# Second attention's and retention's queries and keys: from turned projections to projections by tokens, turned through HBM

## The chip, the cores and the metric

One NeuronCore of a Trainium2 chip runs the whole program. The metric is device microseconds from the start of the program to its end, the median of three runs. Nothing is shared with other cores; HBM is read and written by this core's 16 DMA engines alone.

## The reference

Two layers (D = 1024, 256 tokens, float32), each a mixer and an MLP. The mixer projects the normalised input once into thirteen pieces and feeds three branches:

```python
p = rms_norm(x, g) @ w_in
cq, ckv, k_rope, mq, mk, mv, rq, rk, rv, rg, g_mla, g_moba, g_ret = split(p)
o_mla  = mla_branch(cq, ckv, k_rope, ...)             # first attention, 8 heads
o_moba = moba_branch(mq, mk, mv, cos, sin)            # second attention, 8 heads of 64, partial rotary
o_ret  = retention_branch(rq, rk, rv, rg, ..., cos, sin)   # retention, 4 heads of 64, full rotary
x = x + (sigmoid(g_mla) * (o_mla @ w_a) + sigmoid(g_moba) * (o_moba @ w_b) + sigmoid(g_ret) * (o_ret @ w_c)) @ w_out
x = x + squared_relu(rms_norm(x, g2) @ w_up) @ w_down
```

The change concerns `mq`, `mk` (256 tokens x 512 columns each) and the pair `rq, rk` (together 512 columns): how they are projected, scaled by each token's 1/rms, brought into a layout with the head dimension on the partitions (what the scores need), and rotated (`x1*cos - x2*sin`, `x1*sin + x2*cos`: each element needs its partner from the other half of the rotary dimension).

## The kernel before, in words

**Arithmetic.** Every fp32 product is three TensorE passes: both operands are split into a high part (fp32r) and a low rest, and hi x hi, lo x hi and hi x lo are added in one PSUM bank. Weights arrive by SP's DMA queue as 512 KB tiles `raw` (L218), ScalarE makes the high part `whi` (L284), VectorE the rest `wlo` (L286). There are 7 `raw` tiles and 6 each of `whi` and `wlo`, filled in the order of `weight_plan`.

**Two ways to project.** *By tokens* (`project`, matmuls at L305 to L307, weights moving): 128 activations' columns are loaded into the array, 512 weight columns stream past; for 256 tokens, 512 columns and 8 slices of D that is 2 x 8 x 3 = 48 matmuls of 512 columns, into two `acc` banks. *Turned* (`project_turned`, weights loaded, L504 to L526): for each of 4 blocks of 128 columns, 8 matmuls at L520 stream the high and low parts of 256 tokens side by side (512 columns), and 8 at L522 the high part against `wlo` (256 columns). Both ways stream the same 24,576 columns. In layer 0 `mq` shares the start-up loop over the 8 slices of D with the first attention's columns (`start`; L897 and L899 are its turned matmuls, L905 to L908 the other branch's).

**What a turned projection needs after.** Each block is joined from the two halves of its bank: ScalarE copies one (`second`, L502), VectorE adds (`qkraw`, L502). Tokens are on the free axis, so 1/rms is needed as a row: `stats_row` turns it with TensorE (L456, two transposes a layer) and copies it (`rrow`, L445), and `tables` multiplies it into the rotary tables (`tab`, L533). Rotary partners lie 32 partitions away; `swapped` (L544) copies them with four DMAs of 64 KB within SBUF per pair of blocks. GpSimd rotates the second attention's (`rope_turned`, L556 and L559), VectorE retention's (L1123, L1124).

**The order of the work.** Units of the program (`prog`) stand in a list, extra steps are hung on units with `at(slot(unit, n), ...)`, and a scheduler with its own timeline gives every engine one fixed order; `behind`, `issue_after` and `keep_in_program_order` pin single instructions. An engine executes its order strictly, and so does SP, which issues nearly all DMAs: an issue that waits holds back every later one. The mixer's units run: `start` or `b0`/`mq`, `mk`, then `mv` with the first attention's up-projections between (`qrope`, `qnope`, `kvup`), the gates `gmla`, `gmoba`, then `rqk`, `rv`, `rg`, `gret`, the branch projections, `w_out`. The softmax work of both attentions (L604 to L627, probabilities turned through HBM by L659 and L667) is spread over VectorE and ScalarE under the gates and retention's projections. The first attention's queries `Q` (L1033, L1034) wait for a rotary part `qr` (L1012) and its partner copies `qkoth<-qr` (L544 too); its scores are L1057. Retention's scores are L591 into `ps_r`, read by L1139 into `retA`, used by `ret_values` (L1147 to L1149, `por`).

**Turning through HBM** exists already for the MLP: VectorE transposes 32 x 32 blocks (L335, `hblocks`), one 512 KB DMA writes them to a scratch tensor in HBM (`bounce`, L349), four DMAs of 128 KB read them back turned (`hturned`, L355).

Of the kernel before, what the change touches and what calls it, by code (L numbers as in the profile page):

```python
# [14 lines left out]
P = 128  # L15
# [57 lines left out]
def weight_plan():  # L73
# [7 lines left out]
    def turned(key, cols):  # L81
        for n in range(4):
            block((*key, n), "w_in", KD, cols[P * n : P * n + P], KD)

# [3 lines left out]
    for l in range(L):  # L88
        if l == 0:

            for i in range(2):
                plan.append(((l, "mq", i), "w_in", (0, 1), C_MQ[256 * i : 256 * i + 256]))
            plan.append(((l, "b0", 0), "w_in", (0, 1), C_MLA))
            for k in range(1, KD):
                plan.append(((l, "b0mq", k), "w_in", (k, 1), [*C_MLA, *C_MQ]))
        else:
            block((l, "b0"), "w_in", KD, C_MLA, 2)
            turned((l, "mq"), C_MQ)
        turned((l, "mk"), C_MK)
# [15 lines left out]
        turned((l, "rqk"), C_RQK)  # L115
# [41 lines left out]
def trunk(ctx: ExitStack, tc: tile.TileContext, gx, wts, consts, gfin, gn, xtok, out):  # L157
# [113 lines left out]
    def fetch(key):  # L271
# [10 lines left out]
        parts = (slice(0, 416), slice(416, sz)) if key[1] == "b0mq" else (slice(0, sz),)  # L282
# [82 lines left out]
    class Normed:  # L365
# [87 lines left out]

    def along_free(r, pb):
        for t in range(NT):
            nc.tensor.transpose(pb[:, S + P * t : S + P * t + P], r[:, t : t + 1].to_broadcast([P, P]), ident)  # L456
        return pb[:, S : 2 * S]
# [29 lines left out]
    def project_t(l, key, n, xn, o):  # L487

        wh, wl = load_w(l, key, n, 0)
        for k in range(KD):  # L490
            xh, xl = xn.k(k)
            three(o, wh[:, k, :], wl[:, k, :], xh, xl, k == 0, k == KD - 1)

    def joins(done):

        pair = []

        def join(n, acc):
            if n % 2 == 0:
                pair.append(w2k("qkraw"))  # L500
            second = sb.tile([P, S], F32, name="second", tag="relu", bufs=3)
            both = nc.scalar.copy(second, acc[:, S : 2 * S]), nc.vector.tensor_add(  # L502
                halves(pair[-1])[:, n % 2, :], acc[:, 0:S], second
            )  # L504
            if n % 2:
                done(n // 2, pair[-1])
            return both

        return join

    def project_turned(l, key, xn, done):


        join = joins(done)

        def unit(n):
            wh, wl = load_w(l, key, n, 0)
            acc = acc_tile()
            for k in range(KD):
                nc.tensor.matmul(acc, wh[:, k, :], xn.both(k), start=k == 0, stop=False)  # L520
            for k in range(KD):
                nc.tensor.matmul(acc[:, 0:S], wl[:, k, :], xn.k(k)[0], start=False, stop=k == KD - 1)  # L522
            joined = join(n, acc)
            if key == "rqk" and n:
                behind[l, *(("rv", 3), ("rg", 0), ("rope",))[n - 1]] = joined

        for n in range(4):
            prog.append(((key, n), lambda n=n: unit(n)))

    def tables(xn, tab, engine):  # L530

        o = sb.tile([P, 2 * S], F32, name="tab", bufs=1)
        mul = engine.tensor_mul(halves(o), halves(tab), xn.row[:, None, :].to_broadcast([P, 2, S]))  # L533
        if engine is nc.vector:
            tc.keep_in_program_order(mul)
        return o
# [11 lines left out]

    def rope_turned(raw, tab, engine, late=False):

        other = swapped(raw, late)
        o = sb.tile([P, 2 * S], F32, name="qkT", bufs=4)
        cos, sin = (tab[:, S * i : S * i + S][:, None, :].to_broadcast([P, 2, S]) for i in range(2))
        jobs = [(engine, halves(o), halves(raw), cos), (nc.gpsimd, halves(other), halves(other), sin)]
        for on, *operands in jobs[::-1] if late else jobs:
            mul = on.tensor_mul(*operands)  # L556
        if late:
            tc.keep_in_program_order(mul)
        engine.tensor_add(o, o, other)  # L559
        return halves(o)  # L560
# [216 lines left out]
    begin((0, "mq", 0), "w2k", W2K, nc.scalar)  # L777
    begin((0, "mq", 1), "w2k", W2K)
# [17 lines left out]
    begin((0, "mk", 0, 0))  # L796
# [28 lines left out]
    def layer(l, xn, before):  # L825
# [52 lines left out]
        def start(k, mq):  # L878

            if k == 0:  # L880
                b0.extend(misc_tile("b0") for _ in range(NT))
                mq.extend(acc_tile() for _ in range(4))
            before(k)
            ah, al = xn.k(k)
            if k == 0:
                ws = [load_w(l, "mq", i) for i in range(2)]
                wq = [[w[:, 0, P * i : P * i + P] for w in two] for two in ws for i in range(2)]
                wb = [w[:, 0, :] for w in load_w(l, "b0", 0)]
            else:
                w = load_w(l, "b0mq", k)  # L890
                wq = [[part[:, 0, 416 + P * n : 416 + P * n + P] for part in w] for n in range(4)]
                wb = [part[:, 0, 0:416] for part in w]

            def turned_part(part, ns):
                for n in ns:
                    if part == 0:
                        nc.tensor.matmul(mq[n], wq[n][0], xn.both(k), start=k == 0, stop=False)  # L897
                    else:
                        nc.tensor.matmul(mq[n][:, 0:S], wq[n][1], ah, start=False, stop=k == KD - 1)  # L899
# [10 lines left out]
            if k < KD - 1:  # L910

                for part in range(2):
                    for job in (turned_part, b0_part) if k == 0 else (b0_part, turned_part):
                        job(part, range(4)) if job is turned_part else job(part)
            else:

                join = joins(moba_pair("mq"))
                for part in range(2):
                    turned_part(part, [0])
                for part in range(2):  # L920
                    b0_part(part)
                for n in range(1, 4):
                    for part in range(2):
                        turned_part(part, [n])

                have(1)
                for n in range(4):
                    behind[l, "mk", 1, 0] = behind[l, "mk", 2, 0] = join(n, mq[n])
# [3 lines left out]
        def moba_pair(key):  # L932
            def done(i, raw):
                mqkv[key, i] = raw

            return done

        def moba_tables():
            mqkv["tab"] = tables(xn, TAB, nc.vector)

        def moba_rope(key, i):
            qkT[key][i] = rope_turned(mqkv[key, i], mqkv["tab"], nc.gpsimd, l == 0)

        if l:
            project_turned(l, "mq", xn, moba_pair("mq"))
# [5 lines left out]
            at(slot("mq", 2), xn.stats_row)  # L951
        else:
# [7 lines left out]
            at(slot("start", KD - 1), xn.stats_row)  # L960
        project_turned(l, "mk", xn, moba_pair("mk"))
# [81 lines left out]
        at(slot("mk", 1) if l else slot("gmla0", 1), moba_tables)  # L1043
# [703 lines left out]
```

## Time and profile before

| | us |
|---|---|
| median of 3 runs (lowest, highest) | 803.86 (803.32, 804.36) |
| span of the profiled execution | 801.8 |
| TensorE busy | 795.0 (99% of the span) |
| VectorE busy | 672.4 (84%) |
| ScalarE busy | 489.7 (61%) |
| GpSimd busy | 72.4 (9%) |

The profiler's span covers the instructions; a timed run of this kernel lasts 2.1 us longer by the median (803.86 less 801.8). The granted TensorE clock reads 9 (90% or more) in all 40 slices of the span. Busy TensorE time is that of overlapping matmuls: the distance of one start to the next (227 ns in a run of 512-column matmuls) is what a matmul costs, not its mean duration of 390 ns.

### The profile page before, as it was taken

The page shows a single profiled execution, that of the slowest core. Times are in us where ns is not written, and L with a number is a line of the kernel's source. Part 1 is how long each engine was busy: PE and PEld are TensorE (multiplying, and loading weights), DVE is VectorE, ACT ScalarE, POOL GpSimd, SP SyncE. Part 2 cuts the span into 40 slices and gives each one's busy share as a digit, 9 for nine tenths or more (in the row PEclk, how much of TensorE's full clock was granted, in tenths as well). Part 3 has the DMA queues.
Part 4 walks back from the last instruction along what each step waited for, and adds up shares of the span by engine and source line. Part 5 has one row for each costly group of instructions (what it writes and reads, how often), then busy time and mean ns, then how long its engine had stood idle before and what let it go on. Part 6 is the DMA issues. An engine that isn't in the chain of part 4 may idle for free.

```text
span 801.8 us, 11409 instructions
## 1 busy us (share of the span) xinstructions
PE 795.0 (99%) x3915; PEld 665.1 (83%) x3915; DVE 672.4 (84%) x1128; ACT 489.7 (61%) x758; POOL 72.4 (9%) x61
## 2 busy tenths in 40 slices
PE   9999999999999999999999999999999999999997
PEld 7888887888888888888898888888888888888885
DVE  6859998978888888887798987888698878899785
ACT  7786664653557666666486756655545666667562
POOL 0200810000030000000024330000000300000000
PEclk9999999999999999999999999999999999999999
DMA  9975788975677776787747689687665678788751
GB/s 337 344 238 193 233 270 295 269 264 171 218 232 236 270 214 251 256 271 225 252 149 240 184 231 328 226 261 241 218 221 190 193 259 280 228 284 324 260 174 54
DMA packets 68411, 192.12 MB, mean 240 GB/s; under 512 B 8320, under 2 KB 24832, under 8 KB 68352
## 3 DMA queue, kind: packets, MB, share of 16 engines
q1 hardware_dynamic: 67776, 190.52, 72.5%
q10 hardware_dynamic: 576, 0.87, 0.3%
q8 instruction: 31, 0.51, 0.3%
q14 instruction: 28, 0.23, 0.1%
HBM read 168.81 MB, written 18.87 MB: 234 GB/s over the span
## 4 chain that ended last, share of the span: by engine, by line
PE 98%; ACT 1%; DVE 1%; issue 0%; DVEq 0%
PE acc L305 17%; PE acc L307 17%; PE acc L306 17%; PE pup L306 8%; PE pup L305 8%; PE pup L307 8%; PE acc L1304 6%; PE acc L520 4%; PE acc L522 2%; PE ps_s L1057 1%; PE acc L897 1%; PE po L685 1%; PE ps_s L591 1%; PE warm L805 0%; PE acc L899 0%; PE po L687 0%
## 5 line engine op out<-in xcount | busy, mean ns | idle before, releaser
L284 ACT ACTIVATE whi<-raw 128x1024 fp32r<-128x1024 f32 (+3 forms) x263 | 265.0, 1020 | 165.8 <-PE acc L307 89.9
L286 DVE TENSOR_TENSOR wlo<-raw,whi 128x1024 fp32r<-128x1024 f32 (+3 forms) x263 | 315.9, 1218 | 55.1 <-ACT whi L284 54.1
L305 PE MATMUL acc<-whi,xs 128*128 128x512 f32 (+1 forms) x304 | 119.4, 394 | 0.2 <-DVE qkraw L502 0.2
L306 PE MATMUL acc<-wlo,xs 128*128 128x512 f32 (+1 forms) x304 | 117.8, 388 | 0.0
L307 PE MATMUL acc<-whi,xs 128*128 128x512 f32 (+1 forms) x304 | 117.6, 388 | 0.0
L306 PE MATMUL pup<-wlo,xs 128*128 128x512 f32 x256 | 99.8, 390 | 0.0
L307 PE MATMUL pup<-whi,xs 128*128 128x512 f32 x256 | 99.6, 389 | 0.0
L305 PE MATMUL pup<-whi,xs 128*128 128x512 f32 x256 | 99.4, 389 | 0.0
L307 PE MATMUL acc<-whi,sq 128*128 128x512 f32 x184 | 71.8, 390 | 0.0
L305 PE MATMUL acc<-whi,sq 128*128 128x512 f32 x184 | 71.8, 390 | 0.0
L306 PE MATMUL acc<-wlo,sq 128*128 128x512 f32 x184 | 71.6, 389 | 0.0
L305 PEld LDWEIGHTS acc<-whi,xs 128*128 128x128 f32 x304 | 57.0, 188 | 13.0 <-issue 0.8
L307 PEld LDWEIGHTS acc<-whi,xs 128*128 128x128 f32 x304 | 57.1, 188 | 11.3
L306 PEld LDWEIGHTS acc<-wlo,xs 128*128 128x128 f32 x304 | 57.1, 188 | 10.8
L307 PEld LDWEIGHTS pup<-whi,xs 128*128 128x128 f32 x256 | 48.0, 188 | 9.9
L306 PEld LDWEIGHTS pup<-wlo,xs 128*128 128x128 f32 x256 | 48.1, 188 | 9.8
L305 PEld LDWEIGHTS pup<-whi,xs 128*128 128x128 f32 x256 | 47.9, 188 | 9.9
L613 ACT ACTIVATE prob<-prob,smx 128x128 f32<-128x128 f32 x64 | 28.3, 444 | 30.3 <-DVE smx L610 30.3
L396 POOL TENSOR_TENSOR sqsum<-sqsum,xsq 128x256 f32<-128x256 f32 x16 | 18.2, 1139 | 310.7 <-DVE sqsum L394 298.7
L307 PEld LDWEIGHTS acc<-whi,sq 128*128 128x128 f32 x184 | 34.5, 188 | 7.7 <-DVE sq L326 0.6
L520 PE MATMUL acc<-xs,whi 128*128 128x512 f32 x160 | 40.6, 393 | 0.0
L306 PEld LDWEIGHTS acc<-wlo,sq 128*128 128x128 f32 x184 | 34.5, 188 | 7.2
(277 smaller groups left out, 1383.0 us busy)
## 6 DMA issues: line engine op xcount, KB each, us to landing
raw<-wts SPq DMA_DIRECT2D x264, 512.0 KB, 5.2
bounce<-hblocks SPq DMA_DIRECT2D x16, 512.0 KB, 3.8
hturned<-bounce SPq DMA_DIRECT2D x64, 128.0 KB, 3.1
pbounce<-blocks SPq DMA_DIRECT2D x8, 768.0 KB, 5.9
probT<-pbounce SPq DMA_DIRECT2D x32, 192.0 KB, 5.6
qkoth<-qkraw SPq DMA_DIRECT2D x48, 64.0 KB, 4.7
raw<-wts SPq DMA_DIRECT2D x5, 464.0 KB, 6.0
raw<-wts SPq DMA_DIRECT2D x4, 416.0 KB, 4.8
```

The lines of the kernel that those rows point to most:

```text
L284: fetched.append(nc.scalar.activation(hi[:, cs], raw[:, cs], AF.Copy))
L286: nc.vector.tensor_sub(lo[:, cs], raw[:, cs], hi[:, cs].bitcast(F32))
L305: nc.tensor.matmul(o, ah, bh, start=start, stop=False, **more)
L306: nc.tensor.matmul(o, ah, bl, start=False, stop=False, **more)
L307: nc.tensor.matmul(o, al, bh, start=False, stop=stop, **more)
L396: (nc.gpsimd if n < self.on_pool else nc.vector).tensor_add(self.sum, self.sum, sq)
L520: nc.tensor.matmul(acc, wh[:, k, :], xn.both(k), start=k == 0, stop=False)
L522: nc.tensor.matmul(acc[:, 0:S], wl[:, k, :], xn.k(k)[0], start=False, stop=k == KD - 1)
L591: mm = nc.tensor.matmul(bank[:, o], a[rows, sa], b[rows, sb_], start=True, stop=True)
L613: nc.scalar.activation(p[:, a:b], p[:, a:b], AF.Exp, bias=m[:, 2 + i : 3 + i], scale=d**-0.5, accum_out=m[:, 4 + i : 5 + i])
L685: nc.tensor.matmul(dst, vh, pT[h + j][0], start=True, stop=False)
L1304: nc.tensor.matmul(o, a, b, start=half == 0 and i == 0, stop=4 * half + n == KD and i == len(jobs) - 1)
```

## The change

The six turned projections (`mq`, `mk`, `rqk` in both layers) become projections by tokens. Their weights are now blocked like the others (two slices of D by 512 columns). ScalarE copies the two finished banks out with the token's 1/rms as the scale (`rows`, L881 and L1053 of the new file), VectorE transposes 32 x 32 blocks (L331), one DMA writes 512 KB to HBM (L478), and eight of 128 KB read it back (L483): four give the turned matrix (`raw`), four the same with neighbouring groups of 32 exchanged (`oth`, the rotary partners). `stats_row`, `tables`, `joins` and the SBUF partner copies of these three go; the partner copies of the first attention's `qr` stay. The rotation is done on the re-read matrices with unscaled tables. Of the pins by `behind` around `mk`, `rv`, `rg` and the rotations, most go.

```diff
-        turned((l, "mk"), C_MK)
+        block((l, "mk"), "w_in", KD, C_MK, 2)
...
-        turned((l, "rqk"), C_RQK)
+        block((l, "rqk"), "w_in", KD, C_RQK, 2)
...
-        def stats_row(self):
-
-            pb = along_free(self.r, self.ps)
-            self.row = sb.tile([P, S], F32, name="rrow", bufs=1)
-            nc.scalar.activation(self.row, pb, AF.Copy)
...
-            for k in range(KD):
-                nc.tensor.matmul(acc, wh[:, k, :], xn.both(k), start=k == 0, stop=False)
-            for k in range(KD):
-                nc.tensor.matmul(acc[:, 0:S], wl[:, k, :], xn.k(k)[0], start=False, stop=k == KD - 1)
-            joined = join(n, acc)
...
+    def exchanged(rows, name, tags):
+
+        blocks = blocks_tile(name)
+        for t in range(NT):
+            turn_row(blocks, t, rows[t])
+        bounce = dr.tile([P, 4 * S], F32, name="bounce", bufs=2)
+        nc.sync.dma_start(bounce, blocks)
+        both = [wp.tile([P, 4 * S], F32, name=name + part, tag=tag, bufs=1) for part, tag in zip(("raw", "oth"), tags)]
+        for flip, dst in enumerate(both):
+            for b in range(4):
+                src = bounce.rearrange("(a p) (b r) -> b p a r", a=4, b=4)[b ^ flip]
+                nc.sync.dma_start(dst[32 * b : 32 * b + 32, :].rearrange("p (a r) -> p a r", a=4), src)
+        return both
...
+            def mq_part(part):
+                for a in (ah, al) if part == 0 else (ah,):
+                    for t in range(NT):
+                        first, stop = k == 0 and part == 0 and a is ah, k == KD - 1 and part == 1
+                        nc.tensor.matmul(mq[t], a[:, P * t : P * t + P], wq[part], start=first, stop=stop)
...
+        def exchange(key, accs):
+
+            rows = [w2k("rows") for _ in range(NT)]
+            for t in range(NT):
+                nc.scalar.activation(rows[t], accs[t], AF.Copy, scale=xn.col[t])
+            mqkv[key] = exchanged(rows, key, ("tsums", "thi") if key == "mk" else ("tlo", "exch"))
...
-            project_turned(l, "mq", xn, moba_pair("mq"))
+            project(l, "mq", xn, 512, lambda accs: exchange("mq", accs))
...
-        project_turned(l, "mk", xn, moba_pair("mk"))
+        project(l, "mk", xn, 512, lambda accs: exchange("mk", accs))
...
-                at(slot("mk", 1 + 2 * i), lambda i=i: moba_rope("mq", i))
+                at(slot("mv", 2 * i), lambda i=i: moba_rope("mq", i))
...
-        project_turned(l, "rqk", xn, ret_pair)
-        at(slot("rqk", 1), ret_tables)
+        project(l, "rqk", xn, 512, ret_exchange)
```

Counted over the program, TensorE loses 192 turned matmuls of 512 columns (160 at L520, 32 at L897), 192 of 256 (160 at L522, 32 at L899) and 4 transposes, and gains 288 of 512. VectorE loses 24 additions and 4 table products and gains 12 block transposes; ScalarE loses 24 copies of 128 x 256 and 2 of a row and gains 12 of 128 x 512. SP loses 48 copies of 64 KB and gains 6 writes of 512 KB and 48 reads of 128 KB. GpSimd has as many rotations as before.

The scheduler moves other work with it. SP's queue in layer 1, from the last weights of the keys to the first softmax's turning, before (`qkoth<-qr` are the partners of the first attention's queries, `qkoth<-qkraw` those of the second's):

```order
L544 DMA qkoth<-qkraw 32x512 x4
L218 DMA raw<-wts 128x1024 x2
L544 DMA qkoth<-qkraw 32x512 x4
L218 DMA raw<-wts 128x1024 x2
L544 DMA qkoth<-qr 32x512 x4
L218 DMA raw<-wts 128x1024 x6
```

and with the change:

```order
L478 DMA bounce<-mqblocks 128x1024
L483 DMA mqraw<-bounce 32x4x256 x4
L483 DMA mqoth<-bounce 32x4x256 x4
L213 DMA raw<-wts 128x1024 x4
L478 DMA bounce<-mkblocks 128x1024
L213 DMA raw<-wts 128x1024
L483 DMA mkraw<-bounce 32x4x256 x4
L483 DMA mkoth<-bounce 32x4x256 x4
L509 DMA qkoth<-qr 32x512 x4
L213 DMA raw<-wts 128x1024 x9
```

The partners of the first attention's queries now stand behind the write of the second attention's keys and all eight reads of it. On VectorE in layer 0, where retention's queries and keys come out, before (`prob`, `smx`, `blocks` are the softmax, `omlal` the first attention's output):

```order
L502 TENSOR_TENSOR qkraw<-acc,second 128x256
L627 STREAM_TRANSPOSE blocks<-prob 128x3x4x32 x2
L1123 TENSOR_TENSOR qkoth<-qkoth,tab 128x512
L1123 TENSOR_TENSOR qkT<-qkraw,tab 128x512
L1124 TENSOR_TENSOR qkT<-qkT,qkoth 128x512
L286 TENSOR_TENSOR wlo<-raw,whi 128x1024 x2
L326 TENSOR_TENSOR omlal<-po,omlah 128x512 x2
```

and with the change, first where the blocks are transposed, then, behind four scores' softmax, where the rotation stands:

```order
L282 TENSOR_TENSOR wlo<-raw,whi 128x1024 x6
L331 STREAM_TRANSPOSE rqkblocks<-rows 128x4x4x32 x2
L579 STREAM_TRANSPOSE blocks<-prob 128x3x4x32 x2
L322 TENSOR_TENSOR omlal<-po,omlah 128x512 x2
...
L499 TENSOR_TENSOR qkT<-rqkraw,dec 128x512 x2
L574 TENSOR_SCALAR prob<-prob,smx 128x128
L574 TENSOR_SCALAR prob<-prob,smx 128x256
L568 RECIPROCAL smx<-smx 128x2
L499 TENSOR_TENSOR rqkoth<-rqkoth,dec 128x4x4x32
```

The rotation moved from ahead of that softmax's scores into the middle of its normalisation; retention's scores on TensorE moved with it, from the middle of `rg` to the first matmul behind `rg`.

## Rows read from the trace of the kernel before

**Rows 1.** The page: busy time by engine, and the chain by engine.

```profile
PE 795.0 (99%) x3915; PEld 665.1 (83%) x3915; DVE 672.4 (84%) x1128; ACT 489.7 (61%) x758; POOL 72.4 (9%) x61
...
PE 98%; ACT 1%; DVE 1%; issue 0%; DVEq 0%
```

**Rows 2.** The chain of waits, 24 to 52 us: start, length, what.

```profile
25.52 1.85 PE acc L520 x8
27.37 0.95 PE acc L522 x8
...
44.88 0.66 PE pct L975 x6
```

**Rows 3.** Two stretches of TensorE: length, busy time (records), clock, DMA share, GB/s.

```profile
25.52:36.69 11.17, 11.17 (x65) 1.00 0.89 293
36.69:44.88 8.19, 8.19 (x38) 1.00 1.00 388
```

**Rows 4.** TensorE's timeline from 115 to 119 us, then the chain there.

```profile
117.55 0.50 PE L305 MATMUL acc<-whi,xs 128*128 128x512 f32 x1 [0.24 <-DVE qkraw L502]
...
117.16 0.35 DVE qkraw L502
```

**Rows 5.** The joins of the turned blocks (tile second): ns min/median/max, first and last start.

```profile
L502 ACT COPY second<-acc x24: 351/372/396, 23.2 to 514.3; 128x256 f32<-128x256 f32 x24
L502 DVE TENSOR_TENSOR qkraw<-acc,second x24: 409/418/425, 23.6 to 515.5; 128x256 f32<-128x256 f32 x24
```

**Rows 6.** ScalarE copying a 512-column bank; VectorE's block transposes; their write's landing.

```profile
L1108 ACT ACTIVATE rv<-acc,ms x4: 668/670/673, 139.5 to 531.8; 128x512 f32<-128x512 f32 x4
...
L335 DVE STREAM_TRANSPOSE hblocks<-relu x32: 666/704/714, 243.8 to 771.4; 128x512 f32<-128x512 f32 x32
...
DMA to landing us min/median/max: 2.6/3.8/5.0
```

**Rows 7.** SP's waits (total, times, longest); its issues of turned reads and their landing.

```profile
SPq L355 <- DMA bounce<-hblocks: 50.9, 16, 4.6
...
L355 SPq DMA_DIRECT2D hturned<-bounce x64: 318/423/1785, 248.9 to 776.1; - x64
...
DMA to landing us min/median/max: 2.5/3.1/4.6
```

**Rows 8.** VectorE's timeline, 38 to 46 us: the first attention's latent, layer 0.

```profile
39.59 1.24 DVE L864 TENSOR_SCALAR c<-c,ssc,ms 128x256 f32<-128x256 f32 x4
```

**Rows 9.** The first attention's rotary queries (tile qr): ns min/median/max, landing.

```profile
L544 SPq DMA_DIRECT2D qkoth<-qr x8: 513/590/872, 54.1 to 440.5; - x8
L1033 DVE TENSOR_TENSOR Q<-qr,qkoth x4: 685/690/1662, 59.4 to 450.3; 64x512 f32<-64x512 f32 x4
...
L1030 DVE TENSOR_TENSOR qr<-qr,K x2: 693/974/1254, 58.1 to 442.6; 128x512 f32<-128x512 f32 x2
...
DMA to landing us min/median/max: 2.0/2.2/2.9
```

**Rows 10.** VectorE's weight rests of all shapes: ns min/median/max, first and last start.

```profile
L286 DVE TENSOR_TENSOR wlo<-raw,whi x263: 418/1219/2316, 4.3 to 782.0; 128x1024 fp32r<-128x1024 f32 x120, 128x512 fp32r<-128x512 f32 x8, 128x832 fp32r<-128x832 f32 x2, 128x256 fp32r<-128x256 f32 x1
```

**Rows 11.** The chain, 100 to 152 us, around retention's projections.

```profile
106.17 1.81 PE acc L520 x8
...
123.28 0.58 PE po L685 x4
...
126.04 1.51 PE ps_s L591 x16
```

**Rows 12.** VectorE's softmax steps, groups by shape: count, busy us, mean ns, idle before.

```profile
L627 DVE STREAM_TRANSPOSE blocks<-prob 128x384 f32<-128x384 f32 x32 | 17.8, 568 | 0.2
...
L622 DVE TENSOR_SCALAR prob<-prob,smx 128x256 f32<-128x256 f32 x20 | 6.9, 347 | 0.0
...
L622 DVE TENSOR_SCALAR prob<-prob,smx 128x128 f32<-128x128 f32 x20 | 5.4, 272 | 0.3
```

**Rows 13.** Who waited for rotary partners (tile qkoth): us, times.

```profile
DVE qkoth L1123: 2.4, 1
```

More of the change, by code (lines that the diff above doesn't have):

```diff
@@ L89, in weight_plan @@
         if l == 0:
-            for i in range(2):
-                plan.append(((l, "mq", i), "w_in", (0, 1), C_MQ[256 * i : 256 * i + 256]))
+            plan.append(((l, "mq", 0), "w_in", (0, 1), C_MQ))
             plan.append(((l, "b0", 0), "w_in", (0, 1), C_MLA))
@@ L530, in tables @@
[L530 to L536, printed above, removed]
+    def exchanged(rows, name, tags):
[10 more added lines that the diff above has]
+        return both
@@ new lines, in rope_turned @@
+    def rope_turned(both, tab, i, engine, pins=((), ())):
+        o = sb.tile([P, 2 * S], F32, name="qkT", bufs=4)
+        wide = o.rearrange("p (j t a e) -> p j t a e", j=2, t=NT, a=4)
+        raw, other = (w.rearrange("p (a j t e) -> p j t a e", a=4, j=4, t=NT)[:, 2 * i : 2 * i + 2] for w in both)
+        cos, sin = (
+            tab[:, S * k : S * k + S].rearrange("p (t a e) -> p t a e", t=NT, a=4)[:, None].to_broadcast([P, 2, NT, 4, 32])
+            for k in range(2)
+        )
+        for on, dst, src, by, after in ((engine, wide, raw, cos, pins[0]), (nc.gpsimd, other, other, sin, pins[1])):
+            with ExitStack() as pinned:
+                for ins in after:
+                    pinned.enter_context(tc.issue_after(ins.ins))
+                (engine if engine is nc.vector else on).tensor_mul(dst, src, by)
+        engine.tensor_add(wide, wide, other)
+        return halves(o)
@@ L547, in swapped @@
         return other
[L549 to L560, printed above, removed]
     def rope(xv, c0, s0, t, n, h):
@@ L881, in start @@
                 b0.extend(misc_tile("b0") for _ in range(NT))
-                mq.extend(acc_tile() for _ in range(4))
+                mq.extend(acc_tile() for _ in range(NT))
             before(k)
@@ L885, in start @@
             if k == 0:
-                ws = [load_w(l, "mq", i) for i in range(2)]
-                wq = [[w[:, 0, P * i : P * i + P] for w in two] for two in ws for i in range(2)]
+                wq = [w[:, 0, :] for w in load_w(l, "mq", 0)]
                 wb = [w[:, 0, :] for w in load_w(l, "b0", 0)]
@@ L890, in start @@
                 w = load_w(l, "b0mq", k)
-                wq = [[part[:, 0, 416 + P * n : 416 + P * n + P] for part in w] for n in range(4)]
+                wq = [part[:, 0, 416:928] for part in w]
                 wb = [part[:, 0, 0:416] for part in w]
[L894 to L899, printed above, removed]
+            def mq_part(part):
[3 more added lines that the diff above has]
+                        nc.tensor.matmul(mq[t], a[:, P * t : P * t + P], wq[part], start=first, stop=stop)
             def b0_part(part):
@@ L1110, in ret_done, with ret_exchange @@
             return done
[L1112 to L1125 removed]
+        def ret_exchange(accs):
+            rows = [w2k("rows") for _ in range(NT)]
+            for t in range(NT):
+                nc.scalar.activation(rows[t], accs[t], AF.Copy, scale=xn.col[t])
+            rqkv["both"] = exchanged(rows, "rqk", ("tsums", "thi"))
+        def ret_rope(i):
+            tab = rqkv["dec"][:, RT_H * 3 * P :]
+            rT.append(rope_turned(rqkv["both"], tab, i, nc.vector, ((), behind["po"][1:] if i else ())))
         rT, or_ps, aT, rg, oret, oret_T = [], [], {}, {}, [], []
@@ L1598, in before @@
                 if i == 2:
-                    behind[l + 1, "mq", 0, 0] = turned(3)
+                    behind[l + 1, "mq", 0] = turned(3)
                 if i == 7:
```

86 lines of the change are left out of this document (12 added, 74 removed).

## The prediction

> **What bounds the kernel now.** The page comes first: TensorE is busy 99% of the span, and the chain that ends last runs over TensorE for 98% of it [rows 1]. The reader should see that there is almost no waiting to win: what changes the time is the length of TensorE's own stream, plus whatever new wait the change puts into it. The chain at the start of layer 0 shows what that stream is made of: in a turned block 8 matmuls of 512 columns take 1.85 us, 231 ns each, and 8 of 256 take 0.95 us, 119 ns each [rows 2]. The only wait of a turned projection that reaches TensorE stands at 117 us: retention's values wait for the last join [rows 4]. The profiled span is 801.8 us, 2.1 us under the median run; the sum below is a difference, taken off the median of 803.86 as off the span. About 0.2%, 1.6 us, is what a measurement of this kernel can tell from no change.
>
> **The change part by part.** *The matmuls.* The four turned blocks of layer 0's keys fill the stretch from 25.52 to 36.69, 11.17 us for 64 matmuls, at full clock; the next stretch holds 36 matmuls of 512 columns by tokens in 8.19 us, 227.5 ns each [rows 3]. By tokens a projection is 48 of these: 48 x 0.2275 = 10.92 us, 0.25 less. The columns are the same; the gain is that 119 ns for 256 columns is 5 ns over half of 227.5, and that the turned 512-column ones cost some 3 ns more. I take layer 0's start alike, so six projections give 6 x 0.25 = -1.5 us. The upper end comes from the projection that starts at 106.17 [rows 11] and ends, its wait included, at 117.55 [rows 4]: 11.38 us, 0.46 over 10.92, 2.8 us for six.
>
> The Trainium skill, TensorE: Matmul & The Clock Gate, section Back-to-back issue gap, speaks against a gain: it gives an isolated matmul N/2.4 + 2.5 ns, so 216 ns for 512 columns and 109 for 256. By it, an estimate, a turned projection costs 32 x 216 + 32 x 109 = 10.4 us and one by tokens 48 x 216 = 10.4 us too. The trace does not agree: its 256-column matmuls cost 119 ns and its 512-column ones 227.5 or 231. I go by the rows.
>
> *The transposes.* Four go. Six of the same shape take 0.66 us [rows 2], 0.11 each: -0.44 us.
>
> *The wait at 117 us.* TensorE sat idle 0.24 us there [rows 4]. By tokens the values take two other banks of the four and wait for no join: -0.24 us. Together -2.2 us.
>
> *ScalarE and VectorE.* The joins removed are 24 x 0.37 = 8.9 us on ScalarE and 24 x 0.42 = 10.0 on VectorE [rows 5]; added are 12 copies of 0.67 = 8.0 us and 12 transposes of 0.70 = 8.4 [rows 6]. Both engines get slightly less to do; hidden behind TensorE, worth nothing. The rotations stay, on GpSimd and VectorE.
>
> *SP.* One exchange holds SP's queue for the landing of its write, 50.9/16 = 3.2 us in the mean, and 8 issues of 0.42 [rows 7], 6.6 us in all, in which no weights are issued. Six split weight tiles are 6 x 12 matmuls x 0.2275 = 16.4 us of TensorE work: that covers it, and the MLP's exchanges (with four reads) do the same without a wait. Without that cover each us of delay would cost one. The two halves of the first weights travel on the same two queues as before; only the first two matmuls of 0.23 could wait for the second half, 0 to 0.5 us, and I take 0.
>
> *Layer 0's latent, moved earlier.* VectorE finished it at 39.59 + 1.24 = 40.8 us [rows 8] and TensorE turned it at 44.88 [rows 2]. In the new order its transposes stand behind the first matmul after the keys, at 25.52 + 10.92 + 0.23 = 36.7. If VectorE were no earlier, that is a wait of 4.1 us. But the joins that stood ahead of it are gone: from the end of the start-up loop at 25.52 the new order holds, up to the finished latent, four weight rests of 1.22 and a half one [rows 10], two transposes of 0.70 [rows 6] and the scaling of 1.24: 8.2 us, which leaves 3.0 for some fifteen steps on 32 columns or fewer. I take 0; ends 0 and 4.1.
>
> *Layer 1's first queries, moved back.* Their partner copies now stand behind the keys' write and eight reads, and behind those copies the next nine weight tiles. From the keys' last matmul: two ScalarE copies 1.3, two transposes 1.4 [rows 6], the write 3.2, eight issues 3.4 [rows 7], four partner copies 2.4, landing 2.2, two products of 0.97, four additions of 0.69 [rows 9], one weight rest of 1.22 between [rows 10]: 19.8 us. TensorE has 69 matmuls of 512 columns and 48 of 256 until the scores: 69 x 0.2275 + 48 x 0.119 = 21.4 us. That leaves 1.6 us. Ends: 0 and 5.9, which adds to 19.8 the longest landings (5.0 for the write, +1.8; 2.9, +0.7), the longest products (1.25, +0.6), addition (1.66, +1.0) and rest (2.32, +1.1) and such a rest ahead of the transposes, +2.3: 27.3. The long VectorE operations are those beside GpSimd's rotations, and these now fall there. I take 0.3, near the medians.
>
> *Retention, moved into the softmax.* From its last matmul: copies 1.3, transposes 1.4 [rows 6], two weight rests 2.4 [rows 10], write 3.2, nine issues 3.8, landing 3.1 [rows 7], four products and two additions at 0.69 like those of the queries, 4.1, and among these the normalisation of four scores: four times 0.62 of scaling, two or three transposes of 0.57 [rows 12] and one weight rest, with the reciprocals some 5.7: 25.0 us. TensorE first does 97 matmuls by tokens, 22.1, the output from 123.28 to 126.04, and a score group of 1.51 [rows 11]: 26.4 us. Behind the late products on VectorE wait the weight rests of `gret` and then `retA`. Before, one such product already waited 2.4 us for its partners [rows 13] without holding TensorE. I take 0 of ends 0 and 1.5 a layer (write waited for 4.6 and reads landing after 4.6 us [rows 7], +2.9, less 1.4 of spare).
>
> The sum: -2.2 + 0.3 = -1.9 us: 801.8 becomes 799.9 in the profile, and the median run 802.0.
>
> **The rivals.** *Small waits eat the gain.* Retention's trip takes its longest landings in one layer, +1.5, and layer 1's queries find a slowed rest of 2.32 in front, +0.7 over their spare. For it: 1.4 and 1.6 us of spare are little beside sums of 20 to 25 us made of medians; against: almost no wait stands in the trace of a plan equally tight. Time: 803.86 - 2.2 + 2.2 = 803.9, no change.
>
> *Only columns count.* If the extra 5 ns of a 256-column matmul are hidden when the stream is otherwise free, the projections give nothing: 803.86 - 0.44 - 0.24 = 803.2. Against it: 11.17 us for a stretch with no idle time in it [rows 3]. The formula of the Trainium skill's page named above would give this too.
>
> *Layer 1's queries come late: slower.* The place is the first score of the first attention in layer 1; SP cannot issue their partners before the keys' write has landed, and one VectorE slowed by GpSimd's rotation of the second queries does the rest. Past 21.4 us each us is paid by TensorE; past 25.2 us (21.4 + 2.2 + 1.6) the kernel is slower by over 0.2%. At 26 us, short of the upper end of 27.3: 803.86 - 2.2 + 4.6 = 806.3. For it: GpSimd's rotations fall just there; against: the medians end at 19.8. A latent of layer 0 that is not earlier gives nearly the same, 803.86 - 2.2 + 4.1 = 805.8.
>
> *More than the sum.* Every projection saves 0.46: 803.86 - 2.8 - 0.44 = 800.6.
>
> **How the numbers follow.** The forecast, with waits up to 0.6 us, 0.45; more than the sum 0.08; together faster 0.53. Small waits 0.27 and columns only 0.08: within 0.2%, 0.35. Late queries or a late latent 0.12: slower. The range reaches from 800.6 to 804.8, where waits of 3.1 us end; above it lies most of the slower case, below it next to nothing.
>
> **What would show it.** Right: in the profile after, no idle time of TensorE over 0.5 us apart from the start, 48 matmuls of a projection in 10.9 us, four transposes a program fewer, the span near 799.9. Layer 1's first scores tell on the late queries: an idle time there released by VectorE's `Q`. An idle time at the transposes of the latent near 36.7, at `ps_r` or at `por` names the others. The prediction is wrong if the matmuls by tokens cost over 230 ns in these six projections, or if the waits add up to more than 0.6 us.

## The result, and the profile after

The changed kernel takes 813.6 us (median of 4 runs, 811.8 to 815.0); the kernel before, beside it on the same chip, 803.6 (803.2 to 804.4). The ratio is 1.0123, 95% interval 1.0111 to 1.0135: slower by 10 us, where 802.0 was forecast, in a range of 800.6 to 804.8. The profiled execution's span is 811.4 us, 9.6 over that of before.

The page after: busy time by engine, then the chain that ended last, by engine.

```profile
PE 798.2 (98%) x3815; PEld 660.4 (81%) x3815; DVE 663.8 (82%) x1112; ACT 488.6 (60%) x744; POOL 72.0 (9%) x61
...
PE 81%; DMA 7%; DVE 5%; ACT 2%; SPq 2%; issue 1%; POOL 0%; DVEq 0%; ACTq 0%
```

The chain tells more than the busy share. Before, 98% of it ran over TensorE [rows 1]; now 81%, and 14% over DMA, VectorE and SP's queue (SyncE in the expectations). Where it leaves TensorE, the view of waits says: what TensorE waited for, total us, times, longest.

```profile
PE ps_s L995 <- DVE Q L972: 3.7, 2, 2.7
PE por L1080 <- DVE retA L1072: 0.9, 2, 0.6
PE acc L301 <- ACT th L675: 0.8, 2, 0.4
...
PE ps_s L995 <- DVE Q L973: 0.8, 1, 0.8
```

The first line is the first attention's scores waiting for the rotary queries `Q`, 2.7 in layer 0 and 1.0 in layer 1; the next two are retention, once per layer; the last is the second group of scores in layer 0. They add up to 6.2 us, and the span grew by 9.6: a wait costs more than its length here. TensorE's timeline at layer 0's first scores (start, us, idle before), and layer 1's:

```profile
62.55 0.39 PE L301 MATMUL acc<-whi,xs 128*128 128x512 f32 x1
65.59 0.89 PE L995 MATMUL ps_s<-KK,Q 128*128 128x128 f32 x4 [2.66 <-DVE Q L972]
67.26 3.29 PE L995 MATMUL ps_s<-KK,Q 128*128 128x128 f32 x8 [0.77 <-DVE Q L973]
...
463.99 3.05 PE L995 MATMUL ps_s<-KK,Q 128*128 128x128 f32 x16 [1.05 <-DVE Q L972]
466.69 0.58 PE L301 MATMUL acc<-whi,xs 128*128 128x512 f32 x1
```

The same chain piece by piece in layer 0 (start, us):

```profile
70.61 1.62 PE ps_s L995 x4
72.23 0.43 PE acc L302
72.65 0.43 PE acc L303
...
73.47 0.24 PE acc L302
```

In layer 1 sixteen score matmuls take 466.69 - 463.99 = 2.70 us, in layer 0 72.23 - 65.59 = 6.64. Without a wait layer 0's scores would have begun at 62.78 and, with the three matmuls behind them at 0.23 each, ended at 66.18; the next matmul starts at 73.47, 7.3 us later. VectorE and GpSimd in the same stretch show why:

```profile
59.14 0.69 DVE L969 TENSOR_TENSOR qr<-qr,K 128x512 f32<-128x512 f32 x1 [2.28 <-DMA qkoth<-qr]
59.75 1.79 DVE L969 TENSOR_TENSOR qkoth<-qkoth,K 128x512 f32<-128x512 f32 x1
61.46 2.32 DVE L282 TENSOR_TENSOR wlo<-raw,whi 128x1024 fp32r<-128x1024 f32 x1
63.81 1.64 DVE L972 TENSOR_TENSOR Q<-qr,qkoth 64x512 f32<-64x512 f32 x1
65.48 1.64 DVE L973 TENSOR_TENSOR Q<-qr,qkoth 64x512 f32<-64x512 f32 x1
67.14 1.65 DVE L972 TENSOR_TENSOR Q<-qr,qkoth 64x512 f32<-64x512 f32 x1
68.82 1.64 DVE L973 TENSOR_TENSOR Q<-qr,qkoth 64x512 f32<-64x512 f32 x1
...
59.24 1.75 POOL L499 TENSOR_TENSOR qkT<-mkraw,TAB 128x512 f32<-128x512 f32 x1
60.95 1.75 POOL L499 TENSOR_TENSOR qkT<-mqraw,TAB 128x512 f32<-128x512 f32 x1
62.66 3.91 POOL L499 TENSOR_TENSOR mkoth<-mkoth,TAB 128x512 f32<-128x512 f32 x2
```

Each addition takes 1.64 us instead of 0.69 [rows 9], the rest 2.32 instead of 1.22 [rows 10]; the two engines take turns. GpSimd rotates the second attention's queries and keys here; in the kernel before it began at 82.56, behind the first softmax. The Trainium skill, SBUF — State Buffer, section "SBUF: two separate sides", has the rule: a VectorE operation with two inputs in SBUF and a GpSimd operation that reads SBUF share one pair of ports, and whichever starts first has it for its whole instruction while the other is blocked. The rows agree in kind: each addition takes 0.95 us longer than alone. That is less than the 1.25 to 1.29 that a rotation takes undisturbed (E1), so the wait is not a rotation's whole recorded length.

The 7.3 us of layer 0 then fall into three. The scores begin at 65.59 instead of 62.78: 2.8. The three later groups of four are paced by the additions, 70.61 - 65.59 = 5.0 instead of 3 x 0.68: 3.0. The rest is the clock; the windows of TensorE (length, busy time of PE, PEld, DVE, ACT, POOL, granted clock, DMA share, GB/s):

```profile
62.50:66.00 3.50, 0.84 (x5) 0.45 (x5) 3.44 (x3) 0.32 (x1) 3.50 (x3) 1.00 0.97 351
66.00:68.00 2.00, 1.23 (x6) 0.85 (x5) 1.97 (x2) 0.00 (x0) 2.00 (x2) 0.62 0.29 117
68.00:72.00 4.00, 3.89 (x12) 2.35 (x10) 3.94 (x3) 0.00 (x0) 4.00 (x4) 0.50 0.00 0
72.00:74.00 2.00, 2.00 (x7) 1.57 (x6) 2.00 (x2) 0.00 (x0) 1.81 (x1) 0.67 0.32 35
```

After a stretch with 0.84 us of work in 3.5, the granted clock fell to 0.50, the 1.2 GHz level, until about 73 us: the last group takes 1.62 instead of 0.68, and three matmuls 0.43, 0.43 and 0.39 instead of 0.23: 1.5 us.

Retention, on TensorE's and VectorE's timelines:

```profile
129.28 0.65 PE L637 MATMUL po<-probT,vml 128*64 128x256 f32 x4
...
125.62 1.23 DVE L282 TENSOR_TENSOR wlo<-raw,whi 128x1024 fp32r<-128x1024 f32 x1 [2.02 <-ACT whi L280]
127.76 1.23 DVE L282 TENSOR_TENSOR wlo<-raw,whi 128x1024 fp32r<-128x1024 f32 x1 [0.92 <-ACT whi L280]
130.48 1.23 DVE L282 TENSOR_TENSOR wlo<-raw,whi 128x1024 fp32r<-128x1024 f32 x1 [1.49 <-ACT whi L280]
131.62 1.30 DVE L331 STREAM_TRANSPOSE rqkblocks<-rows 128x512 f32<-128x512 f32 x2
```

ScalarE had copied the rows by 124.6, and the block transposes come 7 us later. Two things stand ahead of them. In VectorE's order there are three weight rests, which wait for ScalarE's high parts, and these for buffers that TensorE gives back at its own pace; the last ends at 131.7. And the transposes write into a buffer of the tag `probT` (`blocks_tile`), which TensorE's matmuls of the first attention's output (`po`, reading `probT`) must give back. E3 shows this second wait by itself: there the release comes 1.6 us after the first of these matmuls, which here would be at 130.9, an estimate. So the rests cost some 0.7 of the 7 us, and the buffer the other 6.3. The write that follows lands after 4.9 us, where the prediction took 3.2.

### The profile page after: what moved, and what is told of

It reads as the page before. It is cut to its first block, busy times and chain, and to the rows that moved or that the text cites. A ratio compares the mean times of both kernels' runs of the same rounds, so it can differ in the third digit from the quotient of the medians.

```text
span 811.4 us, 11168 instructions
## 1 busy us (share of the span) xinstructions
PE 798.2 (98%) x3815; PEld 660.4 (81%) x3815; DVE 663.8 (82%) x1112; ACT 488.6 (60%) x744; POOL 72.0 (9%) x61
## 4 chain that ended last, share of the span: by engine, by line
PE 81%; DMA 7%; DVE 5%; ACT 2%; SPq 2%; issue 1%; POOL 0%; DVEq 0%; ACTq 0%
PE acc L301 16%; PE acc L303 15%; PE acc L302 15%; PE pup L301 8%; PE pup L302 8%; PE pup L303 8%; PE acc L1233 6%; DMA raw<-wts 3%; DVE wlo L282 2%; PE ps_s L995 2%; DMA bounce<-rqkblocks 1%; SPq L483 1%; ACT whi L280 1%; DMA rqkoth<-bounce 1%; DMA xrow<-xtok 1%
## 5 line engine op out<-in xcount | busy, mean ns | idle before, releaser
L282 DVE TENSOR_TENSOR wlo<-raw,whi 128x1024 fp32r<-128x1024 f32 (+3 forms) x263 | 311.7, 1202 | 68.8 <-ACT whi L280 66.9
L301 PE MATMUL acc<-whi,xs 128*128 128x512 f32 (+1 forms) x384 | 150.2, 393 | 0.8 <-ACT th L675 0.8
L302 PE MATMUL acc<-wlo,xs 128*128 128x512 f32 (+1 forms) x384 | 150.3, 392 | 0.0
L303 PE MATMUL acc<-whi,xs 128*128 128x512 f32 (+1 forms) x384 | 149.0, 389 | 0.0
L301 PEld LDWEIGHTS acc<-whi,xs 128*128 128x128 f32 x384 | 72.2, 188 | 16.7 <-ACT th L675 1.3
L303 PEld LDWEIGHTS acc<-whi,xs 128*128 128x128 f32 x384 | 72.3, 188 | 14.4
L302 PEld LDWEIGHTS acc<-wlo,xs 128*128 128x128 f32 x384 | 72.4, 189 | 14.2
L392 POOL TENSOR_TENSOR sqsum<-sqsum,xsq 128x256 f32<-128x256 f32 x16 | 18.3, 1141 | 303.1 <-ACT xs L317 164.8
L303 PEld LDWEIGHTS acc<-whi,sq 128*128 128x128 f32 x184 | 34.5, 188 | 7.8 <-DVE sq L322 0.6
L301 PEld LDWEIGHTS acc<-whi,sq 128*128 128x128 f32 x184 | 34.6, 188 | 7.0
```

The lines of the kernel that those rows point to most:

```text
L282: nc.vector.tensor_sub(lo[:, cs], raw[:, cs], hi[:, cs].bitcast(F32))
L301: nc.tensor.matmul(o, ah, bh, start=start, stop=False, **more)
L302: nc.tensor.matmul(o, ah, bl, start=False, stop=False, **more)
L303: nc.tensor.matmul(o, al, bh, start=False, stop=stop, **more)
L392: (nc.gpsimd if n < self.on_pool else nc.vector).tensor_add(self.sum, self.sum, sq)
```

## The experiments

Each run is named by its label (there is no E4). Times are medians, beside the kernel before on the same chip (803.4 to 803.8 throughout). "Fence" is a GpSimd addition on two columns that reads what GpSimd shall wait for.

**E1: layer 0's rotations behind the last `Q`.** The other engines keep their order.

```diff
-            qkT[key][i] = rope_turned(mqkv[key], TAB, i, nc.gpsimd)
+            qkT[key][i] = rope_turned(mqkv[key], TAB, i, nc.gpsimd, ((behind["Q"],),) * 2 if l == 0 else ((), ()))
+                behind["Q"] = nc.gpsimd.tensor_add(fence[0:64, 0:2], last_q, last_q)
```

> In layer 0 GpSimd's rotations wait for the last addition into the first attention's queries (a small GpSimd addition that reads them stands ahead); every other engine keeps its order. Theory 1 (VectorE is slowed by GpSimd beside it): the four additions take 0.69 us instead of 1.64, the idle time ahead of the first scores of layer 0 falls from 2.8 us to under 1, TensorE's clock stays at 1.00 between 66 and 73 us, and the time falls by 6 to 7.3 us, to 806.3 to 807.6. Rival (the partner copies come late from SP's queue): they are issued at the same 55 us, so the idle time stays over 2 us, the clock falls again and the time stays within 2 us of 813.6.

Measured 817.2 (ratio 1.0166, 1.0151 to 1.0181): slower still. The additions took 0.69 each and the scores waited 0.4, as the theory has it. But then the twelve rotations ran without a pause from 66.42 to 81.27, 1.25 to 1.29 each, and one weight rest did not end before they did. The weight rests from 60 to 84 us (min/median/max), and TensorE's longest wait:

```profile
L282 DVE TENSOR_TENSOR wlo<-raw,whi x4: 1212/1222/16026, 61.1 to 82.3; 128x1024 fp32r<-128x1024 f32 x4
...
PE acc L302 <- DVE wlo L282: 7.3, 1, 7.3
```

One rest of 16.0 us instead of 1.22. So GpSimd's place made the wait at the first scores, and another place can cost more than turns do.

**E2: the queries' partner copies ahead of the keys' reads on SP, both layers.** GpSimd is left free.

```diff
             mla["qo"] = swapped(mla["qr"])
+            with tc.issue_after(behind["partners"].ins):
+                for reads in mqkv.pop("later", ()):
+                    reads()
```

> In both layers the partner copies of the first attention's queries are issued ahead of the eight reads of the second attention's keys; GpSimd is free to rotate whenever its inputs are there. Rival (SP's queue): the copies land some 5 us earlier, both waits for queries (2.8 and 1.4 us) and the fall of the clock go, and the time falls by 7.5 to 8.5 us to 805 to 806. Theory 1: VectorE's products and additions still take over 1.2 us each where GpSimd runs beside them, and some of the wait in layer 0 stays; the time falls by 3 to 8 us.

Measured 810.0 (806.3 to 813.0; ratio 1.0084, 1.0055 to 1.0113). In the profile, which is that of its fastest run, the partners landed 2.4 us sooner (the first product at 56.70), and only some of the additions met a rotation:

```profile
59.16 0.69 DVE L985 TENSOR_TENSOR Q<-qr,qkoth 64x512 f32<-64x512 f32 x1
59.88 1.77 DVE L986 TENSOR_TENSOR Q<-qr,qkoth 64x512 f32<-64x512 f32 x1
```

That is help without a cure. Its five runs spread over 6.7 us, which fits additions that are slowed or not by when the reads land; the slower runs were not profiled.

**E3: retention's transposes ahead of the weight rests from the gate's second weights on.**

```diff
-                for ins in behind.get(first, ()):
+                for ins in (*behind.get(first, ()), *behind.get(("turn", *first), ())):
...
+            behind[("turn", TURN_KEY[0], *TURN_KEY[1:])] = [turn]
```

> VectorE's block transposes of retention's queries and keys stand ahead of the three weight rests that wait for buffers; the rest as planned anew. Theory 2 (the exchange starts 7 us late because the transposes stand behind blocked weight rests): the waits at retention's values (0.7 and 0.5 us) and at the gates behind them (0.4 us twice) go, the time falls by 2 to 3.3 us to 810.3 to 811.6. Rival (the trip through HBM itself is too slow): the waits keep half of their size, the time falls by less than 1.5 us.

Measured 815.5 (ratio 1.0153, 1.0137 to 1.0168). The waits at `por` went, and a new one came:

```profile
131.76 1.30 DVE L331 STREAM_TRANSPOSE rqkblocks<-rows 128x512 f32<-128x512 f32 x2 [7.31 <-PE po L641]
...
PE ps_s L997 <- DVE Q L974: 5.6, 2, 4.5
PE acc L301 <- DVE omobal L322: 3.2, 2, 1.6
```

The order is as wanted, but the transposes start no earlier: VectorE stands idle for 7.3 us a layer until TensorE's `po`, which began at 130.13, gives their buffer back, and the weight rests stand behind them. So the theory is wrong in its cause: but for 0.7 us the rests were not what held the transposes. That the waits at `por` still went fits a start 0.7 us earlier, counted from `po`, and a write that landed after 2.6 us instead of 4.9. The second attention's output (`omobal`) was now split late, 1.6 a layer; that the idle time brings this is likely, since VectorE keeps its order, but was not separated. The waits at `Q`, untouched by the edit, were 1.1 longer than after.

**E5: E1 and E3 with the partners first in layer 1 alone.**

> All three together (GpSimd behind the queries in layer 0, partner copies first in layer 1, retention's transposes early in both). If the three account for the loss, the time is 813.6 - 7 - 1.2 - 3 = 802.4, some 1 us under the kernel before (803.6), and the matmuls by tokens are worth what TensorE's start-to-start distances say (1.65 us). If matmuls by tokens were themselves the loss, it stays over 808.

Measured 815.8 (ratio 1.0149, 1.0132 to 1.0166): E1's rest of 16.0 us and E3's waits of 1.6 again. A miss that adds nothing but that both repeat.

**E6: layer 0's rotations about where they stood before.** The fence reads the first attention's gates instead; the second half has a fence of its own. Only GpSimd's order differs from the changed kernel: TensorE, VectorE, ScalarE and SP's DMAs run through the same instructions in the same order.

```diff
+                o, z = sb.tile([P, 8], F32, name="fence", bufs=1), th_mla[i, NT - 1][:, 0:2]
+                fences[i] = nc.gpsimd.tensor_add(o[:, 0:2], z, z)
```

> Only GpSimd's order in layer 0 differs from the changed kernel: its rotations stand behind a small GpSimd addition that reads the first attention's gates (written at 81 us), the second half behind those written near 94. Theory 1 (the loss at 60 to 75 us is GpSimd's early rotations beside VectorE's additions, and the fall of the granted clock behind that wait; they are harmless where they stood before): Q additions 0.69 each, done near 64.5, idle time before the first scores at most 0.6, nothing new at 81 to 105; 813.6 - 6.5 = 807. Theory 2 (SyncE's late reads of the partners are the loss): the additions start at 62 to 63 as in the first experiment, but the wait stays above 2 us; 812 to 813.6. Theory 3 (twelve rotations starve VectorE wherever they stand): one weight rest of 7 us or more at 81 to 100 and an idle time of TensorE behind it; 811 to 816.

Measured 807.35 (ratio 1.0047, 1.0032 to 1.0062): 6.3 us back, as the first theory said. The rotations ran from 75.7 and from 91.9 (before: from 82.6 on), in turns of 2.27 with VectorE, and no wait of TensorE stands there. The partners landed no sooner than after:

```profile
59.69 0.69 DVE L977 TENSOR_TENSOR qr<-qr,K 128x512 f32<-128x512 f32 x1 [3.19 <-DMA qkoth<-qr]
...
60.91 1.22 DVE L282 TENSOR_TENSOR wlo<-raw,whi 128x1024 fp32r<-128x1024 f32 x1
62.16 0.68 DVE L980 TENSOR_TENSOR Q<-qr,qkoth 64x512 f32<-64x512 f32 x1
```

So SP's queue was not layer 0's loss; with the partners this late, TensorE's wait is 0.3. Layer 1's is 1.0.

**E7: E6 and E2 together**, and **E13**, the same kernel for a second profile.

> As the run before, with the queries' partner copies ahead of the keys' reads on SyncE in both layers. Theory 1: both causes of the loss at the first scores are gone: excess at 60 to 75 us under 0.5, layer 1's wait under 0.5; what is left is retention's (about 2.5 us) less the 1.65 saved by the matmuls: 803.4 - 1.65 + 2.5 = 804.3. Theory 2: the partners' place alone made the difference, so the same as the second experiment: 810.0. Theory 3: over 810.

> The seventh experiment's kernel once more, to see where its runs (804.5 to 808.2) differ, since the one profiled was the fastest of them. Theory: this profile shows a wait of 1 to 3 us at layer 1's first scores or at retention that the other profile lacks. Rival: no new wait, only a lower granted clock.

Measured 806.2 (804.5 to 808.2 in 10 runs; ratio 1.0032, 1.0021 to 1.0043), 1.9 over the forecast of the first theory. The profile of E7 was its fastest run, without a wait at `Q`; E13's (span 804.2 to 802.7) has two of 0.8, in layer 1, which is the difference of the spans:

```profile
449.03 1.75 DVE L993 TENSOR_TENSOR Q<-qr,qkoth 64x512 f32<-64x512 f32 x1
...
448.94 2.99 POOL L505 TENSOR_TENSOR qkT<-mkraw,TAB 128x512 f32<-128x512 f32 x2 [6.82 <-DMA mkraw<-bounce]
```

In layer 1 too, rotations meet the additions, two of four in E7 and all four in E13. (E6 and E7 differ by 1.2 us in the median, but the intervals of their ratios overlap.)

**E15: E7 with layer 1's rotations of the keys behind the first gates**, by the same fence.

```diff
-                at(slot("gmla0", 1 + 2 * i), lambda i=i: moba_rope("mk", i))
+                at(slot("gmla1", 1 + i), lambda i=i: moba_rope("mk", i))
```

> The seventh experiment's kernel (all by tokens, late rotations in layer 0, partners first) with layer 1's rotations of the keys behind the first gates. Theory 1: the additions at 0.69, the wait of 0 to 1.9 at layer 1's first scores goes, median 806.1 - 1.2 = 804.9 and the spread halves. Rival: the wait stays, released by the partners' landing; 806.1.

Measured 804.7 (803.9 to 805.4 in 10 runs; ratio 1.0015, 1.0005 to 1.0024): as forecast, the spread included. All six projections are still by tokens here. What TensorE still waits for stands in retention, at `Q` in layer 0, and at a rest of the first weights:

```profile
PE acc L301 <- ACT th L684: 0.8, 2, 0.4
...
PE acc L858 <- DVE wlo L282: 0.7, 1, 0.7
PE por L1101 <- DVE retA L1093: 0.6, 1, 0.6
PE ps_r L552 <- DVE qkT L506: 0.5, 1, 0.5
PE ps_s L1016 <- DVE Q L993: 0.5, 1, 0.5
```

**E8: E7 with retention turned as before, E9: the changed kernel with that alone.** Both bring back `project_turned`, `joins`, `tables` and the row statistics for `rqk`.

> As the run before, with retention's queries and keys computed turned again, as the kernel before does it; queries and keys of the second attention stay by tokens. Theory 1 (retention by tokens costs its waits, 0.7 + 0.6 in layer 0 and 0.5 + 0.6 in layer 1, and saves 2 x 0.25 and two transposes): 1.5 to 2 us less than the run before, 802.5. Rival (retention's waits would come in another place, or the turned matmuls cost what the waits did): within 0.5 of the run before.

> The changed kernel with retention's queries and keys computed turned again, nothing else. Theory 1: the loss of layer 0 and of layer 1's queries stays, only retention's 2.4 us of waits go and some 0.7 of saving: 813.6 - 1.7 = 811.9. Rival (most of the loss is retention's, the early waits being made up for later): below 808.

E8 measured 804.2 (ratio 1.0006, 0.9997 to 1.0016), 2.0 under E7. E9 measured 812.9 (809.7 to 814.0; ratio 1.0104, 1.008 to 1.0128), 0.7 under the changed kernel where 1.7 was expected; its waits at `Q` were 6.0 in sum instead of 4.5, so it cannot settle retention's share. E8 can: most of the loss isn't retention's, some 2 us are, and 2.6 by the medians of the spans (804.35 to 801.7); the difference lies outside the span, of which more below.

**E10: E8 with the queries' reads behind the partners too in layer 0, E14: E10 with layer 1's rotations late.**

> As the kernel with late rotations, partners first and retention turned (804.2), with the reads of the second attention's queries too behind the partner copies in layer 0. Theory 1: the partner copies no longer stand behind eight reads on SyncE, so the wait of 0.45 before layer 0's first scores goes: 803.7, and below 803.5 only if the spread of the runs goes with it. Rival (the partners were not late by SyncE's queue, but by the writes' landings): no change, 804.2.

> The tenth experiment with layer 1's rotations of the second attention's keys behind the first gates (about 466 us), as layer 0's are. Theory 1 (these rotations beside the four additions set layer 1's wait, more or less of it by when the partners land): all four additions at 0.69 in layer 1, and the median comes down to the profile's best, 803.35 - 0.6 = 802.8, ratio 0.9985. Rival (the partners' landing alone): no change, 803.4.

E10 measured 803.35 (ratio 0.9998, 0.9989 to 1.0007) and E14 803.5 (1.0, 0.9991 to 1.0009): no different from the kernel before. E14 missed its 802.8, since there was no wait to win: in E10's profile three of layer 1's four additions still took 1.67 to 1.69, but they began 5.2 us ahead of the scores (445.89 and 451.09), where E13's began 2.9 us ahead of the scores' turn (449.03 and 451.89), and TensorE did not wait. E14's spans are shorter than the kernel before's, 800.7 to 801.5 in 11 runs with a median of 801.0, where that has 801.0 to 802.5 and 801.7; but some 2.5 us of its time lie outside the span (803.19 to 800.7 in the profiled run) and 1.8 of that of before (803.35 to 801.5 in one). All four kernels with retention turned again (E8, E9, E10, E14) have 2.2 to 2.6 us there, E3, E5 and E11 1.9 to 2.2, and all others, the kernel before among them, 1.7 to 1.9. No view shows what they are; that stays open.

**E11: all by tokens with E6's fences, the partners first, and retention's transposes pinned as in E3, one weight earlier.**

> All six projections by tokens, late rotations, partners first (queries' reads too), and retention's two transposes ahead of VectorE's weight rests from the first of the gate's weights on. Theory 1 (retention's waits come from these transposes behind weight rests that wait for buffers): no wait at retention's scores and values in either layer, 1.5 us less than the kernel without this (806.2): 804.7. Rival (the same VectorE work then makes the second attention's output late, as in the third experiment): a wait of 1 to 2 us for omobal per layer, 806 to 808.

Measured 807.1 (ratio 1.0038, 1.0024 to 1.0052): the rival. The waits at `ps_r` and `por` went, two of 1.5 for `omobal` took their place, beside two of 0.8 at `Q`. As in E3, the transposes stood idle for their buffer, 9.1 us in layer 0 and 10.0 in layer 1, until `po`.

**E12: E1 with the second six rotations behind the gates.**

> The first experiment with GpSimd's twelve rotations in two halves of six; the second half stands behind the first gates of the first attention. If VectorE is held off for as long as GpSimd runs without a pause, the weight rest that took 16.0 us takes 7 to 9 and ends with the sixth rotation at about 74, before TensorE runs out of weights: 817.2 - 7 or more = 806 to 810. If the lock is lost for another reason (the first rotation alone, the strided shapes): a rest over 10 us again, or one of 2.3 as elsewhere.

Measured 812.6 (ratio 1.0117, 1.0103 to 1.013). The first half of the expectation came true, the time didn't. The three rests that held 18.3 us in E1 now take 11.0, and the held one goes on once the sixth rotation has ended, at 73.67:

```profile
64.91 10.98 DVE L282 TENSOR_TENSOR wlo<-raw,whi 128x1024 fp32r<-128x1024 f32 x3
...
72.39 1.28 POOL L500 TENSOR_TENSOR qkT<-qkT,mqoth 128x512 f32<-128x512 f32 x1
```

TensorE waited for no rest. But the hold was paid later. VectorE's and ScalarE's work behind it stands 7.4 us later than in E6, whose order is the same on every engine but GpSimd. TensorE ran on until it wanted the banks that ScalarE's gates (`th`) give back, at 98.23 (ScalarE in E6, then ScalarE and TensorE in E12):

```profile
85.98 0.40 ACT L565 ACTIVATE prob<-prob,smx 128x128 f32<-128x128 f32 x1 [6.73 <-DVE smx L562]
...
93.34 0.40 ACT L565 ACTIVATE prob<-prob,smx 128x128 f32<-128x128 f32 x1 [6.73 <-DVE smx L562]
...
98.23 0.80 PE L301 MATMUL acc<-whi,xs 128*128 128x512 f32 x1 [4.39 <-ACT th L675]
```

The place of the later rotations is not the fault. In both kernels six rotations run beside the second softmax, and ScalarE waits 6.73 us for VectorE's maxima; in E6 this costs TensorE nothing. What differs is the 7.4 us. After the wait of 4.39 the granted clock was 0.50 from 98 to 100 and 0.54 from 100 to 103, and TensorE fell back by 2.2 us more. So a delay of VectorE is paid where TensorE first needs what comes of it, here some 30 us behind the hold's start.

## Why the prediction was wrong

**The matmuls: right.** Layer 0's keys by tokens are 48 matmuls from 25.18; the next unit's first starts at 36.08:

```profile
25.18:36.10 10.92, 10.92 (x50) 9.03 (x49) 10.11 (x27) 10.47 (x21) 2.38 (x2) 1.00 1.02 402
```

That is 10.90 us without idle time and at full clock, against 11.17 [rows 3]; 10.92 was forecast. E14 has four such projections and no wait of TensorE but the 0.8 at the warm-up matmuls that the kernel before has too. Its profiled span is 1.1 under that of before, where 4 x 0.25 + 0.24 = 1.2 was due; by the medians of all spans it is 0.7 (E10: 1.0). "Only columns count" is out.

**Layer 0's latent: right.** Its turn stands at 36.31, with no idle time before it. The bound of 4.1 us was not needed.

**"The rotations stay, on GpSimd and VectorE", hidden, worth nothing: the step that failed.** They stay in number, not in place. The diff drops `late`, the pin that held layer 0's rotations in program order, and nothing else kept them from starting as soon as their reads landed, at 50.6 instead of 82.6 us. That put them beside the first queries' additions. Layer 0's 7.3 us are this, and E6, which moves nothing but these rotations, gives 6.3 of the run time back.

**"Layer 1's first queries": right in mechanism, but for one layer of two.** The text named rotations beside additions and long rests, and gave them to layer 1 alone; layer 1 lost 1.05, inside its bounds, and 0 and 1.6 in the two profiles of E7's kernel. Layer 0 has the same additions and had no term at all. The fall of the clock that made 1.5 us more of layer 0's wait was in no rival.

**Retention: 0 taken of 0 to 1.5 a layer; waits of 0.9 a layer came** (`por` and `th`, 1.7 in both; `ps_r` adds 0.2). Inside the range, but not by the sum: that has 2.4 us, "two weight rests", between the rows and the transposes, and it was 7. Three rests stood there, but what was left out is the transposes' buffer, which `po` gives back: without the rests ahead the wait for it was 7.3 and 9.1 us (E3, E11). The prediction counted `po` among TensorE's work and not as what releases the transposes. No run gave them a buffer of their own.

**SP's queue: covered in layer 0, as said.** Partners first gave 1.2 (E6 to E7), not clear of noise; by the waits at `Q` mostly in layer 1. The first weights' halves, "0 to 0.5 us", taken as 0: none after, but 0.4 to 0.7 in the profiles of E1, E6, E11, E12 and E15.

The medians add up: 813.6, with layer 0's rotations late 807.4, partners first 806.2, layer 1's rotations late 804.7. Of the 1.2 left over 803.5, the waits of E15, 3.1 in sum, less 0.2 before, less the 1.5 + 0.44 that the matmuls and transposes were worth, make 1.0; E15's profile is a run 0.5 over its median, so this fits to about half a us. No version tried beats the kernel before by what can be measured.

## What to carry to other kernels

When a change rewrites how data arrive, list what the old code pinned and ask of each unpinned instruction when it can now start at the earliest, and beside whose critical step: work that is "hidden" in total time can still stand in the wrong microsecond. Between GpSimd and VectorE a place matters more than a duration; a fence on a late tile is a cheap way to choose it. And price a step by everything that can release it, not by the medians of what stands ahead of it: when its inputs land, when its engine's order reaches it, and when the buffer that it writes comes free. To pin it earlier in the order helps only where the order was the last of these.

## What the runs showed of the hardware

VectorE can lose its turn for much longer than one instruction. Mostly the two engines alternate: 2.27 us for a rotation of 1.28 and about as much for a rest of 1.22 (E6, and the kernel before from 92 us on). In E1, E5 and E12 GpSimd's rotations went through one after the other at 1.25 to 1.29 while a rest waited for all of them: 16.0 us for twelve, and 8.7 in E12, until the sixth had ended. In each of these the fence had itself just waited for a rest (1.23 us for 64 x 2 elements, where E6's took 0.19 and 0.42), and the next rest and the first rotation started 0.09 us apart. Whether that is what decides between turns and none was not tried.
